# Opening stage of a diffusion backbone layer: tokens fetched first, squares taken per token, half columns first, three DMA queues

## The chip, the cores and the metric

The kernel runs on one core of one Trainium2 chip. The time is that of the core on the device, in microseconds (us): 2735.46 us as the median of 3 runs (2735.38 to 2736.6). A core has five engines with a program each: TensorE (PE), VectorE (DVE), ScalarE (ACT), GpSimd (POOL) and SyncE (SP), which here only issues DMAs. Each runs its own program in order and waits on semaphores for the others.

## The reference

One layer over 1024 latent tokens and 256 context tokens of width 1024, all in float32. Only the first part matters here: nine modulation rows per stream, then a norm with shift and scale, and the first SwiGLU network, whose hidden width is 2816.

```python
mod_lat = (silu(c) @ w_mod + b_mod)            # 9 rows of 1024: ml[0..8]
mod_ctx = (silu(c_ctx) @ w_mod + b_mod)        # mc[0..8]
x  = x  + 0.5 * ml[2] * swiglu(modulate(rms_norm(x,  norm1_g), ml[0], ml[1]), ffn1_w_in, ffn1_w_out)
cx = cx + 0.5 * mc[2] * swiglu(modulate(rms_norm(cx, norm1_g), mc[0], mc[1]), ffn1_w_in, ffn1_w_out)
hx = modulate(rms_norm(x, norm2_g), ml[3], ml[4])
...
return rms_norm(x, final_g)
```

Here `rms_norm(x, g) = x * rsqrt(mean(x*x) + eps) * g`, `modulate(h, shift, scale) = h * (1 + scale) + shift`, and `swiglu` is `(silu(a) * b) @ w_out` with `a, b` the two halves of `h @ w_in`. A convolution branch, attention, their merge and a second SwiGLU follow; they are the same in both kernels.

## The kernel before

**Numbers and products.** Everything is float32. A matrix that goes through PE is split into an upper part (rounded to fp32r, by a CAST on ScalarE) and a lower part (what is left, by a subtraction, mostly on VectorE), and each product term takes three matmuls (`terms`): upper by upper, upper by lower, lower by upper. A split weight lies in a tile `wh` or `wl` (the same thing in two pools of four buffers; the list `WH` says which of the first 16 goes where), its source in a `raw` tile of three buffers.

**Scheme.** The class `Winograd` forms the first network's two columns `a` and `b` of 128 for all 1024 tokens by seven products in place of eight. The 1024 features have an upper half (k 0 to 3) and a lower half (k 4 to 7), the tokens a first half C0 and a second half C1. The right-hand operands `r1` to `r7` are sums of the four blocks of the normed tokens: `r1` is the upper half of C0, `r2` its lower half, and `r3` to `r7` need C1 too. There are 22 units j, each of one column pair. Products 1 and 2 of a unit use column `a` alone; they are made for the first eight units ahead of everything (`start_together`, `AH1 = 8`), for these need only C0. Then each unit makes its products 6, 7, 4 (`second`) and 5, 3 (`third`). From unit 8 on the context's 256 tokens run beside a unit's weights (`SIDE_FROM = 8`); for units 0 to 7 they come in one pass of their own after unit 7.

**Opening.** A modulation half row is written (m, half): m = 1 is the scale, m = 0 the shift, half 0 its first 512 columns. For (1,0) and (0,0) `first_mod` makes both streams' rows on PE (`rawm` is the loaded weight, `silu_c` has two columns). For (1,1) and (0,1) `second_mod` makes the latent's alone, as sums on VectorE (`macc`) and a short product. The context's half of these comes later, in `later_mod`. The tokens of C0 (`xtok`, 128 tokens by 1024) are turned on PE, copied to `x`, squared on ScalarE (`sq`), summed by GpSimd (`sq_acc`), and a product with ones gives the sums per token. `rsqrt_cols` finds the root on VectorE by small steps (`rs_a`, `rs_y`, `rs_t`), and `bcast` turns it into a tile that VectorE multiplies by (`h0`); `shifted` then applies gain and shift on ScalarE, and `keep` splits into `r1`, `r2`. The same is done for C1, whose `norm1` makes `r3` to `r7` with `scaled`, sums and splits on VectorE.

**Work beside the units.** `all_later_mods` is a chain of small steps. After unit j, `STEPS[j]` of them run: none after unit 0, and 6, 6, 6, 7, 7, 8, 8 after units 1 to 7, 48 in all. A `later_mod` pass of one half row has 8 steps with loads and sums on VectorE, then waits, a split, and a short product on PE: 19 steps. The chain begins with (1,1) and (0,1) for the context, then the context's norm `normc` (10 steps; results `h1ch`, `h1cl`, the operands of the context products), then the rows m = 2 and up.

**Order.** All weights, tokens and modulation rows are fetched on SP's queue; the 16 stores of `x` to DRAM (`xd`) are on it too. The code is written in the order of the wanted program, and the tile scheduler then settles each engine's order by a time simulation of its own; on the chip an engine keeps that order.

The order of the opening and of the chain is set by these lines:

```python
    half1.prefetch(8, lo_engines=(dve, pool))
    raws11 = fetch_mod(1, 1)
    t1 = fetch_tokens(C1)
    half1.prefetch(10)
    raws01 = fetch_mod(0, 1)
    tx = fetch_tokens(CC)
    ...
    def all_later_mods():
        yield from later_mod(1, (1,), (1,))
        yield from later_mod(0, (1,), (1,))
        part_gain(gain1["c"], 0, "g1", "c", 4, 8)
        for _ in normc:
            yield
```

Of the kernel before, what the change touches and what calls it, by code (L numbers as in the profile page):

```python
# [18 lines left out]
P = 128  # L19
# [23 lines left out]
WAIT = 4  # L43
AH1, WH = 8, (4, 5, 6, 7, 10, 11, 14, 15)
RESIDENT, AH2, AH3 = 2, 9, 9
# [4 lines left out]
def tile_dit_layer(  # L50
# [249 lines left out]

    def fetch_mod(m, half):
        raws = []
        for kk in range(KD // 2):
            raw = atile("rawm", (P, 2, 512))
            o = m * D + half * 512
            load(out=raw[:], in_=w_mod[0, kk * 256 : (kk + 1) * 256, o : o + 512].rearrange("(a p) n -> p a n", p=P))
            raws.append(raw)
        return raws
# [155 lines left out]
    class Winograd:  # L464
# [6 lines left out]
        def __init__(self, xs, gain, mod, m, pairs, plain=False, ahead=3, side_from=None):  # L471

            self.xs, self.gain, self.mod, self.m, self.plain = xs, gain, mod, m, plain
            self.r = {i: [None] * 4 for i in range(8)}
            self.side_from = side_from  # L480
            self.n_ahead, self.side, self.started, self.n_left = ahead, None, [], 0
            self.n_squares, self.accs = {}, {}
            self.source, self.ready = self.lefts(pairs, side_from), []
# [44 lines left out]
        def norm1(self):  # L528
            y = rstd_cols(self.accs[C1], 512, D)
            yield  # L530
# [44 lines left out]
        def lefts(self, pairs, side_from):  # L575
# [100 lines left out]
        def start_together(self):  # L676

            n = self.n_ahead
            ws = [self.ready.pop(0) for _ in range(8)]
            ps = [ps_s() for _ in range(4)]  # L680

            def together(i, js, ps):
                for k in range(4):
                    for j in js:
                        self.terms(ps[j], ws[2 * j + i - 1], i, k)

            uc = {}
            for js in ((0, 1), (2, 3)):
                together(1, js, ps)
                for j in js:  # L690
                    uc[j] = atile("uc", (P, 2, 512))
                    act.copy(out=uc[j][:, 0], in_=ps[j])
                yield
            for j in range(4, n):
                p1 = self.product(1)
                uc[j] = atile("uc", (P, 2, 512))
                act.copy(out=uc[j][:, 0], in_=p1)
                yield
            for js in ((0, 1), (2, 3)):
                p2 = {j: ps_s() for j in js}  # L700
                together(2, js, p2)
                for j in js:
                    dve.tensor_add(out=uc[j][:, 1], in0=uc[j][:, 0], in1=p2[j])
                    self.started.append((uc[j][:, 0], uc[j][:, 1]))
                yield
            for j in range(4, n):
                dve.tensor_add(out=uc[j][:, 1], in0=uc[j][:, 0], in1=self.product(2))
                self.put_aside(uc[j])
                yield
# [218 lines left out]

    def fetch_tokens(ch):
        s, o, n = ch  # L930
        src = x[0] if s == "l" else ctxt[0]
        toks = []
        for j in range(n // P):
            t = atile("xtok")
            load(out=t[:], in_=src[o + j * P : o + (j + 1) * P, :])
            toks.append(t)
        return toks
# [28 lines left out]

    def squares(ch, turn):

        accs = [ttile("sq_acc")]
        for k in range(KD):  # L970
            run(turn, 1)
            sq = ttile("sq") if k else accs[0]
            act.activation(out=sq, in_=xs(k, ch), func=AF.Square)
            if k == KD - 1:
                accs.append(sq)
            elif k:
                pool.tensor_add(out=accs[0], in0=accs[0], in1=sq)
            yield accs

    run(mod10, 2)  # L980
    for accs in squares(C0, turn_tokens(C0, t0, ("dve", "dve"))):
        pass
# [9 lines left out]
    run(mod00, 1)  # L992
    y = rstd_cols(accs, 512, D)
    run(mod00)
    pr = bcast(y, 512)
    half1.h0 = h0 = [atile("h0", (P, 2, 512)) for _ in range(4)]

    def scaled(k, i):
        dve.tensor_mul(out=h0[k][:, i], in0=xs(k + 4 * i, C0), in1=pr)

    scaled(0, 0)
    scaled(1, 0)
    for k in range(4):
        half1.shifted(h0[k][:, 0], k)
        half1.keep(1, k, h0[k][:, 0])
        if k < 2:
            scaled(k + 2, 0)
# [3 lines left out]
    for k in range(4):  # L1011
        scaled(k, 1)
    run(mod11, 8)
    run(start, 2)
    turned = squares(C1, turn_tokens(C1, t1))
    run(mod11, 1)
    run(turned, 2)
    run(mod11, 1)
    for k in range(6):
        accs = next(turned)  # L1020
        run(mod01, 2 if k < 2 else 1)
    run(start, 2)
    half1.accs[C1] = accs
    norm1 = half1.norm1()
    run(mod11)
    part_gain(gain1["l"], 0, "g1", "l", 4, 8)
    run(mod01, 1)
    run(norm1, 1)
# [4 lines left out]
    run(norm1, 1)  # L1033
    run(start, 1)
    run(norm1, 1)
    run(start, 1)
    for _ in range(3):
        run(norm1, 1)
        run(start, 1)
    run(start)  # L1040
# [764 lines left out]
```

## Time and profile before

| what | before |
|---|---|
| median of 3 runs | 2735.46 us (2735.38 to 2736.6) |
| profiled execution, its span | 2735.6 us |
| PE busy | 2662.7 us, 97% |
| VectorE busy | 2021.2 us, 74% |
| ScalarE busy | 1152.3 us, 42% |
| GpSimd busy | 547.9 us, 20% |
| DMA, mean over the span | 130 GB/s |

The profile is that of one execution. All times in it count from the start of its span. A row of the order of time has the start, the busy time, the engine, the line (always L88, the helper that records every operation), the operation and its tiles (out<-in, buffer numbers left out), partitions by elements, a count, and in brackets the idle time before it with what ended it. Since every operation is at line 88, the tiles' names say which part of the kernel a row is. A row of the stretches has start and end, the length, the busy times, with how many instructions, and the granted clock of PE as a share of full speed. The page's digits show PE's idle time in the opening: 7, 8, 9, 8 tenths busy in the first four slices of 68 us, 9 in nearly all the others.

### The profile page before, as it was taken

The numbers are of one execution on the slowest core, as the hardware profiler recorded it, in microseconds if no ns is written. First come the engines' busy times: TensorE is split into PE (matmuls) and PEld (weight loads), VectorE is DVE, ScalarE is ACT, GpSimd is POOL, SyncE is SP. The second block draws the span as 40 slices with busy tenths as digits, with TensorE's granted clock in tenths as the row PEclk, the third lists the DMA queues.
The fourth block names the chain that finished last, engine by engine and source line by source line (L and its number), as shares of the span: only waits on it lengthen the run. The fifth ranks groups of instructions, "written<-read, shape, count | busy, mean of one in ns | idle before, by whom it ended". The sixth has DMA issues, their size and how long they took to land.

```text
span 2735.6 us, 37415 instructions
## 1 busy us (share of the span) xinstructions
PE 2662.7 (97%) x13629; PEld 2246.2 (82%) x13629; DVE 2021.2 (74%) x3368; ACT 1152.3 (42%) x2293; POOL 547.9 (20%) x419
## 2 busy tenths in 40 slices
PE   7898999999999999999999999999999999999998
PEld 4687988888878877888999888887888788888888
DVE  5887688877778799887578676685548886667885
ACT  4534333333444552333345566674226333334443
POOL 2241122221011024332023111100000442320200
PEclk8899999999999999999999999999999999999999
DMA  8264443434985255443312321001533552328841
GB/s 304 94 203 149 143 133 101 133 107 150 319 235 111 98 163 173 142 127 107 122 39 70 108 80 48 28 32 47 168 108 125 169 169 82 96 85 282 180 89 62
DMA packets 355650, 354.38 MB, mean 130 GB/s; under 512 B 27382, under 2 KB 248712, under 8 KB 355464
## 3 DMA queue, kind: packets, MB, share of 16 engines
q1 hardware_dynamic: 346440, 334.68, 37.5%
q0 software_dynamic: 9024, 17.30, 4.0%
q8 instruction: 107, 1.75, 0.3%
q14 instruction: 79, 0.65, 0.1%
HBM read 287.91 MB, written 63.96 MB: 129 GB/s over the span
## 4 chain that ended last, share of the span: by engine, by line
PE 55%; DVE 4%; ACT 1%; issue 1%; DMA 1%; POOL 0%; DVEq 0%; SPq 0%; POOLq 0%; ACTq 0%
PE ps L88 46%; PE pt L88 5%; PE po L88 4%; DVE wl L88 1%; DVE y L88 0%; DVE macc L88 0%; DVE u L88 0%; DVE ol L88 0%; ACT pts L88 0%; DVE v L88 0%; DVE r L88 0%; POOL s L88 0%; DVE x L88 0%; DVE pts L88 0%; DMA rawm<-in_w_mod_dram 0%
## 5 line engine op out<-in xcount | busy, mean ns | idle before, releaser
L88 PE MATMUL ps<-r,wl 128*128 128x512 f32 x5280 | 1231.3, 392 | 17.9 <-ACT r L88 6.1
L88 PEld LDWEIGHTS ps<-r,wl 128*128 128x128 f32 x5280 | 991.1, 189 | 232.4 <-DVE wl L88 8.7
L88 ACT CAST wl<-s 128x512 fp32r<-128x512 f32 x256 | 158.0, 620 | 344.2 <-PE ps L88 251.2
L88 POOL TENSOR_TENSOR s<-raw 128x512 f32<-128x512 f32 x64 | 99.8, 1559 | 944.0 <-DMA raw<-in_ffn_w_in_dram 575.3
L88 ACT CAST wl<-raw 128x512 fp32r<-128x512 f32 x278 | 171.7, 620 | 266.6 <-PE ps L88 172.8
L88 DVE TENSOR_TENSOR wl<-raw,wl 128x512 fp32r<-128x512 f32 x276 | 198.3, 719 | 80.8 <-ACT wl L88 79.5
L88 DVE TENSOR_TENSOR wl<-s,wl 128x512 fp32r<-128x512 f32 x256 | 222.1, 868 | 10.8 <-ACT wl L88 9.3
L88 POOL TENSOR_TENSOR s<-raw,s 128x512 f32<-128x512 f32 x64 | 104.7, 1636 | 415.3 <-DVE wl L88 415.3
L88 DVE SCALAR_TENSOR_TENSOR macc<-rawm,silu_c,macc 128x512 f32<-128x512 f32 x168 | 144.6, 879 | 9.5 <-DMA rawm<-in_w_mod_dram 8.8
L88 PE MATMUL ps<-wh,r 128*128 128x256 f32 x768 | 141.6, 285 | 0.0
L88 DVE TENSOR_TENSOR pts<-pt,pts 128x512 fp32r<-128x512 f32 x160 | 108.9, 687 | 39.3 <-ACT pts L88 38.4
L88 DVE TENSOR_TENSOR u<-u,ps 128x512 f32<-128x512 f32 x168 | 114.3, 680 | 30.9 <-PE ps L88 30.1
L88 DVE TENSOR_REDUCE m<-ps 128x1 f32<-128x512 f32 (+1 forms) x192 | 111.0, 596 | 30.8 <-PE ps L88 30.0
L88 ACT CAST pts<-pt 128x512 fp32r<-128x512 f32 x160 | 93.3, 594 | 88.7 <-PE pt L88 86.8
L88 PE MATMUL ps<-rh,wl 128*128 128x512 f32 x360 | 123.2, 392 | 2.8 <-ACT rh L88 2.8
L88 ACT CAST rh<-hid 128x512 fp32r<-128x512 f32 x132 | 81.1, 620 | 97.9 <-PE ps L88 78.9
L88 PEld LDWEIGHTS ps<-wh,r 128*128 128x128 f32 x768 | 120.6, 192 | 0.0
L88 PE MATMUL po<-pts,vh 128*128 128x512 f32 x256 | 110.5, 437 | 1.5 <-ACT pts L88 1.5
L88 PE MATMUL ps<-wl,r 128*128 128x256 f32 x384 | 108.8, 283 | 0.0
L88 ACT CAST wh<-raw 128x512 fp32r<-128x512 f32 (+1 forms) x84 | 67.1, 803 | 97.2 <-PE ps L88 76.3
L88 PE MATMUL ps<-kl,qs 128*128 128x512 f32 x384 | 105.3, 397 | 0.0
L88 DVE TENSOR_TENSOR rl<-hid,rh 128x512 fp32r<-128x512 f32 x132 | 90.0, 686 | 20.1 <-PE ps L88 12.2
(281 smaller groups left out, 5112.6 us busy)
## 6 DMA issues: line engine op xcount, KB each, us to landing
raw<-in_ffn_w_in_dram SPq DMA_DIRECT2D x117, 512.0 KB, 5.0
raw<-in_ffn_w_out_dram SPq DMA_DIRECT2D x72, 512.0 KB, 5.6
rawm<-in_w_mod_dram SPq DMA_DIRECT2D x128, 256.0 KB, 4.4
raw<-in_w_in_dram SPq DMA_DIRECT2D x61, 512.0 KB, 3.7
hid<-hd SPq DMA_DIRECT2D x40, 512.0 KB, 7.0
ws<-in_ffn_w_out_dram POOLq DMA_DIRECT2D x30, 512.0 KB, 6.6
hd<-c SPq DMA_DIRECT2D x38, 256.0 KB, 2.0
hd<-u SPq DMA_DIRECT2D x38, 256.0 KB, 2.8
```

The costliest lines, as they stand in the source:

```text
L88: inst = getattr(self.engine, name)(*args, **kw)
```

## The change

The opening is written anew, and one pass of the chain goes:

- **Fetches.** C0's tokens are fetched ahead of (1,0) and (0,0). `load`, `fetch_mod` and `fetch_tokens` take a queue: (1,1), C1's tokens and (0,1) are now issued by ScalarE, the 16 stores of `x` by GpSimd. The context's tokens are fetched later, still on SP.
- **Squares.** `token_rstd` squares a token tile of 1024 on ScalarE, with the row sum in the same instruction (`sqtok`, `rs_a`), straight after it is fetched. `squares`, GpSimd's sums and the product with ones are gone.
- **Scaling.** The broadcast root is copied to SBUF (`pr`). Each turned block is scaled from PSUM into `h0` by VectorE, while ScalarE copies it to `x`.
- **Weights.** The 16 columns for products 1 and 2 are all loaded as halves, the upper halves of the eight pairs first, then the lower ones; before, four were whole columns and came first. `start_together` follows that order: units 0 and 1 together, then one unit at a time. `WH` is adapted.
- **Modulation.** (1,1) is made on PE for both streams (`first_mod`), with the context's gain behind it, so the chain's first pass `later_mod(1, (1,), (1,))` is gone; with the same `STEPS`, all that follows in the chain runs 19 steps earlier. (0,1) is still made by `second_mod`.
- **Second half.** C1's root comes from `token_rstd`; its tokens are turned behind the first lower-half products rather than between the upper ones.

```diff
-    def load(out, in_, pinned=False):
-        inst = sp.dma_start(out=out, in_=in_)
+    def load(out, in_, pinned=False, queue=None):
+        inst = (queue or sp).dma_start(out=out, in_=in_)
...
             n = self.n_ahead
-            m = 4 if self.side_from else n
-            for a, _ in pairs[:m]:
-                yield from map(parts, cols(a))
-            for half in range(2):
-                for a, _ in pairs[m:n]:
-                    yield parts(half_cols(a, half))
+            if self.side_from:
+                for half in range(2):
+                    for a, _ in pairs[:n]:
+                        yield parts(half_cols(a, half))
+            else:
+                for a, _ in pairs[:n]:
+                    yield from map(parts, cols(a))
...
-    raws10 = fetch_mod(1, 0)
     t0 = fetch_tokens(C0)
-    raws00 = fetch_mod(0, 0)
+    raws10, raws00 = fetch_mod(1, 0), fetch_mod(0, 0)
...
+    def token_rstd(toks):
+
+        ss, sq = small("rs_a", 4), atile("sqtok")
+        for j, t in enumerate(toks):
+            act.activation(out=sq[:], in_=t[:], func=AF.Square, accum_out=ss[:, j : j + 1])
+        dve.tensor_scalar(out=ss[:], in0=ss[:], scalar1=D * EPS, scalar2=None, op0=ALU.add)
+        return rsqrt_cols(ss[:], 4)
+
+    half1.prefetch(3)
+    y = token_rstd(t0)
+    raws11 = fetch_mod(1, 1, act)
+    pr = ttile("pr")
+    dve.tensor_copy(out=pr, in_=bcast(y, 512))
+    half1.h0 = h0 = [atile("h0", (P, 2, 512)) for _ in range(4)]
+    run(mod10, 1)
+    for k in range(KD):
+        pt = (ps_o if k % 2 else ps_t)()
+        for j, t in enumerate(t0):
+            transpose(pt[:, j * P : (j + 1) * P], t[:, k * P : (k + 1) * P])
+        act.copy(out=xs(k, C0), in_=pt)
+        dve.tensor_mul(out=h0[k % 4][:, k // 4], in0=pt, in1=pr)
     run(mod10)
     for s in "lc":
         part_gain(gain1[s], 0, "g1", s, 0, 4)
-    half1.prefetch(8, lo_engines=(dve, pool))
-    raws11 = fetch_mod(1, 1)
-    t1 = fetch_tokens(C1)
-    half1.prefetch(10)
-    raws01 = fetch_mod(0, 1)
-    tx = fetch_tokens(CC)
+    t1 = fetch_tokens(C1, act)
+    raws01 = fetch_mod(0, 1, act)
+    half1.prefetch(5, lo_engines=(dve, pool))
...
     start = half1.start_together()
     run(start, 2)
-    mod11, mod01 = second_mod(1, 1, raws11), second_mod(0, 1, raws01)
...
+    mod11, mod01 = first_mod(1, 1, raws11), second_mod(0, 1, raws01)
     run(mod11)
     part_gain(gain1["l"], 0, "g1", "l", 4, 8)
+    part_gain(gain1["c"], 0, "g1", "c", 4, 8)
+    run(start, 1)
+    run(mod01, 8)
+    run(start, 2)
+    half1.rstd1 = token_rstd(t1)
     run(mod01)
     for k in range(4):
         half1.shifted(h0[k][:, 1], k + 4)
         half1.keep(2, k, h0[k][:, 1])
+    run(start, 2)
+    tx = fetch_tokens(CC)
+    run(turn_tokens(C1, t1, ("act", "dve")))
+    norm1 = half1.norm1()
     run(start, 1)
+    run(norm1, 2)
+    for _ in range(4):
+        run(start, 1)
         run(norm1, 1)
...
-            sp.dma_start(out=xd[k, :, ch[1] : ch[1] + 512], in_=xs(k, ch))
+            pool.dma_start(out=xd[k, :, ch[1] : ch[1] + 512], in_=xs(k, ch))
...
     def all_later_mods():
-        yield from later_mod(1, (1,), (1,))
         yield from later_mod(0, (1,), (1,))
-        part_gain(gain1["c"], 0, "g1", "c", 4, 8)
         for _ in normc:
             yield
```

**ScalarE in the opening.** These rows are ScalarE's program from the first modulation row to the splits of the first weights, before; the numbers at names are buffers, and the brackets hold the semaphores that a row waits for (DMAHW: the completion of DMAs).

```order
L88 COPY mrow_139<-ps_130 2x512 [waits PE_49]
L88 ACTIVATE sq_acc_141<-x_147 128x512 [waits DVE_49]
L88 ACTIVATE sq_157<-x_155 128x512 [waits DVE_49]
L88 ACTIVATE sq_167<-x_165 128x512 [waits DVE_49]
L88 ACTIVATE sq_177<-x_175 128x512 [waits DVE_49]
L88 ACTIVATE sq_186<-x_147 128x512
L88 CAST wl_228<-raw_226 128x512 [waits DMAHW0_49]
L88 CAST wl_231<-raw_226 128x512
```

The same place after the change, and, behind the "...", the rows between the third weight's split and the first shift.

```order
L88 ACTIVATE sqtok_146,rs_a_145<-xtok_110 128x1024 [waits DMAHW7_49,Activation_49]
L88 DMA rawm_164<-in_w_mod_dram 128x2x512 [waits DMAHW3_49]
L88 DMA rawm_166<-in_w_mod_dram 128x2x512 [waits DMAHW4_49]
...
L88 CAST wl_142<-raw_140 128x512 [waits DMAHW2_49]
...
L88 DMA xtok_267<-in_x_dram 128x1024 [waits DMAHW3_49]
L88 DMA xtok_269<-in_x_dram 128x1024 [waits DMAHW4_49]
L88 DMA xtok_271<-in_x_dram 128x1024 [waits DMAHW5_49]
L88 COPY x_211<-pt_236 128x512 [waits PE_49]
L88 DMA rawm_273<-in_w_mod_dram 128x2x512 [waits DMAHW6_49]
L88 COPY x_203<-po_229 128x512 [waits PE_49]
```

The squares are now of whole token rows and stand ahead of the weights' splits; twelve DMA issues, each waiting for the transfer eight before it, and the copies of `x` have come into ScalarE's line ahead of the shifts.

**PE at the second token half's norm.** Before, PE's rows around the broadcast of C1's root (`pt_678<-ident,rs_y_639`), which stands ahead of the first product of the lower half (`r_150` is an `r2`):

```order
L88 MATMUL ps_651<-accl_625,ones_r 1x512
L88 MATMUL pt_656<-ident,mrow_654 128x1 x4
L88 MATMUL pt_678<-ident,rs_y_639 128x128 x4
L88 MATMUL pt_939<-ident,xtok_292 128x128
L88 MATMUL pt_939<-ident,xtok_294 128x128
L88 MATMUL ps_683<-r_150_663,wl_231 128x512
L88 MATMUL ps_684<-r_150_663,wl_239 128x512
```

After, the same broadcast (`pt_650<-ident,rs_y_473`; `r_106` to `r_109` are the four `r2`):

```order
L88 MATMUL ps_612<-r_109_513,wl_449 128x512
L88 MATMUL ps_613<-r_109_513,wl_519 128x512 x3
L88 MATMUL ps_655<-r_108_509,wl_539 128x512 x3
L88 MATMUL ps_655<-r_109_513,wl_539 128x512 x3
L88 MATMUL ps_708<-r_106_501,wl_616 128x512
L88 MATMUL pt_650<-ident,rs_y_473 128x128 x4
L88 MATMUL ps_708<-r_106_501,wl_616 128x512 x2
```

It has moved behind the lower-half products of units 0 to 2 and one of unit 3.

**VectorE at the context's root.** Before, the root's first row (`rs_a_1873<-pt_1870`) stands at the end of unit 7, among its last adds to `u` and splits of weights:

```order
L88 TENSOR_TENSOR u_1725<-u_1725,ps_1951 128x512
L88 TENSOR_TENSOR wl_1966<-raw_1926,wl_1966 128x512
L88 TENSOR_SCALAR rs_a_1873<-pt_1870 128x2
L88 TENSOR_SCALAR rs_y_1875<-rs_a_1873 128x2
L88 SCALAR_TENSOR_TENSOR rs_t_1876<-rs_y_1875 128x2
```

After, it stands in unit 5, with the norm's first rows (`nt`) behind it and ahead of the unit's next add (`v_1608`):

```order
L88 TENSOR_TENSOR wl_1628<-s_311_1467,wl_1628 128x512
L88 TENSOR_TENSOR modc<-mcol_1535,bcol 128x4
...
L88 TENSOR_SCALAR rs_a_1567<-pt_1564 128x2
L88 TENSOR_SCALAR rs_y_1569<-rs_a_1567 128x2
...
L88 TENSOR_TENSOR nt_1584<-xc_97,pt_1581 128x256
L88 TENSOR_TENSOR nt_1589<-xc_97,pt_1581 128x256
L88 TENSOR_TENSOR nt_1594<-xc_97,pt_1581 128x256
L88 TENSOR_TENSOR nt_1599<-xc_97,pt_1581 128x256
L88 TENSOR_SCALAR nt_1584<-nt_1584,gain_c,modc 128x256
L88 TENSOR_TENSOR v_1608<-u_1421,ps_1631 128x512
```

The root, its eleven small rows and the context's norm have moved two units ahead, between the adds and splits of units 5 and 6.

More of the change, by code (lines that the diff above doesn't have):

```diff
@@ L43 @@
 WAIT = 4
-AH1, WH = 8, (4, 5, 6, 7, 10, 11, 14, 15)
+AH1, WH = 8, (4, 5, 6, 7, 12, 13, 14, 15)
 RESIDENT, AH2, AH3 = 2, 9, 9
@@ L299, in later_mod, with fetch_mod @@
             yield
-    def fetch_mod(m, half):
+    def fetch_mod(m, half, queue=None):
         raws = []
@@ L305, in fetch_mod @@
             o = m * D + half * 512
-            load(out=raw[:], in_=w_mod[0, kk * 256 : (kk + 1) * 256, o : o + 512].rearrange("(a p) n -> p a n", p=P))
+            src = w_mod[0, kk * 256 : (kk + 1) * 256, o : o + 512].rearrange("(a p) n -> p a n", p=P)
+            load(raw[:], src, queue is not None, queue)
             raws.append(raw)
@@ L528, in norm1 @@
         def norm1(self):
-            y = rstd_cols(self.accs[C1], 512, D)
+            y = self.rstd1 or rstd_cols(self.accs[C1], 512, D)
             yield
@@ L678, in start_together, with together @@
             n = self.n_ahead
-            ws = [self.ready.pop(0) for _ in range(8)]
-            ps = [ps_s() for _ in range(4)]
-            def together(i, js, ps):
+            uc = [None] * n
+            def together(i, js):
+                ps = [ps_s() for _ in js]
+                ws = [self.left() for _ in js]
                 for k in range(4):
[L684 to L690, printed above, removed]
+                    for w, p in zip(ws, ps):
+                        self.terms(p, w, i, k)
+                return zip(js, ps)
+            groups = ((0, 1), *((j,) for j in range(2, n)))
+            for js in groups:
+                for j, p in together(1, js):
                     uc[j] = atile("uc", (P, 2, 512))
-                    act.copy(out=uc[j][:, 0], in_=ps[j])
+                    act.copy(out=uc[j][:, 0], in_=p)
                 yield
[L694 to L708, printed above, removed]
+            for js in groups:
+                for j, p in together(2, js):
+                    dve.tensor_add(out=uc[j][:, 1], in0=uc[j][:, 0], in1=p)
+                    if j < 4:
+                        self.started.append((uc[j][:, 0], uc[j][:, 1]))
+                    else:
+                        self.put_aside(uc[j])
                 yield
@@ L927, in tile_dit_layer, with fetch_tokens @@
     xs, xc = Latents("x"), Context("xc")
-    def fetch_tokens(ch):
+    def fetch_tokens(ch, queue=None):
         s, o, n = ch
@@ L934, in fetch_tokens @@
             t = atile("xtok")
-            load(out=t[:], in_=src[o + j * P : o + (j + 1) * P, :])
+            load(t[:], src[o + j * P : o + (j + 1) * P, :], queue is not None, queue)
             toks.append(t)
@@ L965, in tile_dit_layer @@
     half1 = Winograd(xs, gain1["l"], modl, 0, column_pairs(ffn1_w_in[0], ffn_offsets), ahead=AH1, side_from=SIDE_FROM)
[L967 to L982, printed above, removed]
+    def token_rstd(toks):
[17 more added lines that the diff above has]
+        dve.tensor_mul(out=h0[k % 4][:, k // 4], in0=pt, in1=pr)
     run(mod10)
@@ L1005, in tile_dit_layer @@
         half1.keep(1, k, h0[k][:, 0])
-        if k < 2:
-            scaled(k + 2, 0)
+    half1.prefetch(8, lo_engines=(dve, pool))
     start = half1.start_together()
     run(start, 2)
-    mod11, mod01 = second_mod(1, 1, raws11), second_mod(0, 1, raws01)
[L1011 to L1024, printed above, removed]
+    mod11, mod01 = first_mod(1, 1, raws11), second_mod(0, 1, raws01)
     run(mod11)
     part_gain(gain1["l"], 0, "g1", "l", 4, 8)
-    run(mod01, 1)
-    run(norm1, 1)
+    part_gain(gain1["c"], 0, "g1", "c", 4, 8)
[3 more added lines that the diff above has]
+    half1.rstd1 = token_rstd(t1)
     run(mod01)
```

15 lines of the change are left out of this document (1 added, 14 removed).

## The prediction

> **What bounds the kernel now.** I read the page's head, then busy time in stretches cut where the program's stages begin and end, then the order of time around each gap of TensorE (PE).
>
> ```profile
> span 2735.6 us, 37415 instructions
> ...
> 0.00:44.40 44.40, 28.93 (x103) 12.83 (x103) 22.60 (x47) 14.57 (x25) 13.16 (x15) 0.87 0.98 361
> 44.40:71.40 27.00, 26.43 (x114) 21.30 (x115) 16.32 (x22) 14.42 (x28) 4.62 (x3) 0.90 0.59 196
> 71.40:88.20 16.80, 8.80 (x43) 6.51 (x41) 11.49 (x27) 9.63 (x18) 5.93 (x4) 0.66 0.44 141
> 112.90:127.90 15.00, 11.57 (x42) 7.17 (x40) 14.28 (x19) 5.41 (x10) 8.38 (x4) 0.89 0.57 194
> 180.80:234.00 53.20, 53.05 (x235) 42.79 (x233) 43.36 (x72) 18.69 (x36) 18.72 (x12) 1.00 0.54 167
> 234.00:244.00 10.00, 1.59 (x5) 0.91 (x6) 9.13 (x31) 3.89 (x10) 0.00 (x0) 0.67 0.39 124
> 244.00:320.00 76.00, 71.86 (x571) 70.72 (x571) 46.98 (x78) 35.46 (x68) 6.33 (x4) 0.98 0.49 159
> 320.00:700.00 380.00, 379.66 (x2122) 330.48 (x2121) 295.39 (x453) 128.37 (x231) 84.97 (x52) 1.00 0.41 129
> ```
>
> Columns: stretch, length, busy PE, weight loads, VectorE (DVE), ScalarE (ACT), GpSimd (POOL), granted clock, DMA share, GB/s. PE is the bound from 320 us on (379.66 of 380); what is late there stays late. So the change is worth what it moves in the first 245 us. PE does little useful before 44.4 us, little from 71.4 to 88.2 and almost nothing from 234 to 244. The profiled span, 2735.6, is 0.14 above the median of the runs shown (2735.46), so the sum is made against 2735.6.
>
> ```profile
> 32.29 0.38 PE L88 MATMUL pt<-ones,sq_acc 128*128 128x1 f32 x2 [4.49 <-POOL sq_acc L88]
> 40.47 1.09 PE L88 MATMUL pt<-ident,rs_y 128*128 128x128 f32 x4 [3.69 <-DVE rs_y L88]
> 44.39 1.22 PE L88 MATMUL ps<-r,wl 128*128 128x512 f32 x2 [1.56 <-ACT r L88]
> 88.21 1.22 PE L88 MATMUL ps<-r,wl 128*128 128x512 f32 x2 [1.40 <-ACT r L88]
> 136.96 54.28 PE L88 MATMUL ps<-r,wl 128*128 128x512 f32 x238
> 237.24 0.60 PE L88 MATMUL pt<-ident,rs_y 128*128 128x128 f32 x2 [3.29 <-DVE rs_y L88]
> 241.43 0.58 PE L88 MATMUL ps<-h1ch,wl 128*128 128x256 f32 x1 [3.59 <-ACT h1ch L88]
> 243.59 0.58 PE L88 MATMUL ps<-h1cl,wl 128*128 128x256 f32 x1 [1.58 <-DVE h1cl L88]
> ```
>
> Three waits stand out. The first product starts at 44.39, after GpSimd's sum of squares (4.49) and VectorE's root (3.69). The second half's products start at 88.21. At 234 PE waits for the context norm: 3.29 + 3.59 + 1.58 = 8.5. A 512-wide product matmul takes 54.28 / 238 = 0.228.
>
> **The change, part by part.** The old opening first.
>
> ```profile
> 6.00:50.00 44.00, 33.31 (x114) 16.19 (x115) 27.73 (x52) 15.55 (x27) 14.03 (x10) 0.81 1.06 397
> q1 hardware_dynamic: 11944, 18.21, 98.4%
> 6.33 0.43 SPq L88 DMA_DIRECT2D rawm<-in_w_mod_dram  x1
> ...
> 10.13 0.37 SPq L88 DMA_DIRECT2D rawm<-in_w_mod_dram  x1
> 22.50 2.16 ACT L88 CAST wl<-raw 128x512 fp32r<-128x512 f32 x4
> 6.38 9.85 PE L88 MATMUL ps<-rawm,silu_c 128*2 128x512 f32 x16 [2.51 <-DMA rawm<-in_w_mod_dram]
> ```
>
> *Fetches.* One queue holds the 16 DMA engines full (share 1.06, 397 GB/s). The four issues of SP from 6.33 to 10.13 (first and last shown) stand 1.27 apart: each waits for the transfer eight before it, the first of which is the one PE reads at 6.38. So 512 KB land every 1.27, from 6.3 on. After the change the four token tiles land from 6.3 to 10.1 and the modulation columns (1,0) and (0,0) next; the first split of a weight follows the same twelve transfers, as it does now at 22.5. But ScalarE's queue now puts 2.1 MB of (1,1) beside them. The third half weight is the 9.2nd MB: 8.7 MB after the first tile, 21.9 at 397 GB/s, ends at 28; with (1,1) left behind it would be at 23. I take 26.
>
> The Trainium skill, "DMA: Bandwidth & Descriptors", section "Issuing engines are not separate DMA queues", speaks against the three queues: transfers of SP, ScalarE and GpSimd run on the same 16 engines and interleave, and only issue time is saved. The rows above agree (98.4% with one queue). Were the queues to add bandwidth instead, the weights would come at 23 and the sum below would be 3 lower.
>
> *The first product.* Squares, root, broadcast and the first two of the eight scalings move ahead of the weights: they end near 17, beside the fetches, so GpSimd's sums (4.49) and most of the root's wait go. What is late next is ScalarE's own line. Behind the third weight stand, in its order, 11 casts and copies, 8 DMA issues, 4 shifts and a cast.
>
> ```profile
> 47.22 1.13 ACT L88 CAST wh<-raw 128x512 fp32r<-128x512 f32 x2
> 84.73 2.93 ACT L88 ACTIVATE h<-h,modl,gain_l 128x512 f32<-128x512 f32 x4 [0.87 <-DVE modl L88]
> L88 ACT ACTIVATE ws<-ws x12: 632/1057/1062, 779.3 to 2577.5; 128x1024 f32<-128x1024 f32 x10, 128x512 f32<-128x512 f32 x2
> L88 POOL DMA_DIRECT2D ws<-in_ffn_w_out_dram x36: 1197/1222/1442, 740.3 to 2624.9; - x36
> ```
>
> Sum: 11 x 0.55 = 6.1, 8 x 0.42 = 3.3 (a DMA issued by ScalarE is not in this trace; SP's rows say 0.37 to 0.43, and up to 1.27 when the transfer eight before is late), 2.9 and 0.6: 12.9. The first product starts at 39, against 44.39. The squares with their row sums are not in the trace; the nearest row is 1.06 for a 1024-wide ACTIVATE, and four of them keep pace with tiles 1.27 apart. The 16 stores leave SP's queue for GpSimd's, at 1.2 each, and cost nothing on the path: behind them stand three of its splits, whose lower parts PE reads more than 10 us after the first product's start. Without that cover each would cost 1.2.
>
> *First to second half.*
>
> ```profile
> 70.20 0.93 PE L88 MATMUL pt<-ident,xtok 128*128 128x128 f32 x7
> 86.42 1.29 DVE L88 TENSOR_TENSOR h<-x,pt 128x512 f32<-128x512 f32 x2 [1.27 <-PE pt L88]
> 132.54 0.68 DVE L88 TENSOR_TENSOR r<-nt,r 128x512 fp32r<-128x512 f32 x1
> 86.40:133.20 46.80, 41.97 (x154) 31.53 (x154) 44.72 (x65) 25.53 (x44) 12.59 (x7) 0.85 0.20 68
> 105.07 1.41 DVE L88 TENSOR_TENSOR r<-h,r 128x512 fp32r<-128x512 f32 x1
> ```
>
> From 39 PE does 8 two-row products for (1,1), 9.85 / 16 x 8 = 4.9, 96 matmuls, 21.9, and about 1.5 at half clock: 67. Now this ends at 71.4. Then row, turn, add, 4 shifts and a cast, 4.5: the second half starts near 72, not 88.2. But that is not the gain. The second token half's norm is now broadcast behind 37 of these matmuls (8.4), 16 turns (16 x 0.93 / 7 = 2.1) and a cold start (1.7), so VectorE's first scaling comes at 84, against 86.42.
>
> From there VectorE is the bound, now as after: 65 instructions in 46.8 up to the last operand r of the first unit (133.2), 0.72 each, with some of them stretched (1.41 where 0.68 is usual). The new order has 58: 41.5, so 125.5. PE, done with the second half at 97, waits for it; that wait takes the place of the one at 71. **First term: 125.5 - 133.2 = -7.7.** Between: -13 (weights at 23, 3 less; 0.68 in place of 0.72 each, 2.3 less) and 0 (ScalarE's issues at 1.27 each: 6.9 more).
>
> *The context norm.* The column half (1,1) now comes for both streams at once, so a context pass of 19 steps goes, and the norm, which needed all 48 steps of units 1 to 7, is done by step 29, in unit 5. The gap at 234 goes, and with it the slow start behind it: the mean clock of 0.98 from 244 to 320 is a loss of 0.02 x 76 = 1.5. **Second term: -(8.5 + 1.5) = -10.** With the pass go 2.1 MB of SP's loads and its sums on VectorE, in units 1 to 3, where PE is full anyway: nothing.
>
> *What it is traded for.* The work of that gap, and half of the next modulation row, fall into units 4 to 7, where PE is full.
>
> ```profile
> 237.88 2.74 DVE L88 TENSOR_TENSOR nt<-xc,pt 128x256 f32<-128x256 f32 x8 [0.70 <-PE pt L88]
> 240.53 2.67 DVE L88 TENSOR_SCALAR nt<-nt,gain_c,modc 128x256 f32<-128x256 f32 x8
> 243.12 2.76 DVE L88 TENSOR_TENSOR h1cl<-nt,h1ch 128x256 fp32r<-128x256 f32 x8
> L88 DVE SCALAR_TENSOR_TENSOR macc<-rawm,silu_c,macc 128x512 f32<-128x512 f32 x14 | 13.4, 954 | 1.2 <-DMA rawm<-in_w_mod_dram 1.1
> ```
>
> VectorE gets 2.74 + 2.67 + 2.76 = 8.2 of norm, 2.2 of root (11 at 0.2), 7 more sums of modulation at 0.95 = 6.7 and 1.2 of others: 18.3. It was busy 43.4 of 53.2 there, so 8.5 do not fit. The root also stands in VectorE's line ahead of unit 5's adds: it waits for a sum that PE makes only in unit 5's last product, and behind it are queued the adds that free PE's banks and the splits of unit 6's weights. The splits run some four weights ahead of PE, which may hide part. **Third term: +9**, between 0 (all hidden) and +13.5 (another 5 for the root's wait). The 10 is thus nearly given back.
>
> Sum: 2735.6 - 7.7 - 10 + 9 = **2726.9**.
>
> The Trainium skill, "TensorE: Matmul & The Clock Gate", Part 1, says that an idle window of some 3.4 us puts PE back to half clock. By that rule PE's broken work from 97 to 125 would leave it cold and add about 1.7 to the sum; the stretch from 112.9 to 127.9, also broken, kept 0.89, so I add nothing.
>
> **The rivals.** *The backlog is hidden:* four weights of lead and unit 4's slack take the third term to 2, and the time is 2719.9. For it: VectorE has idle time in units 0 to 4. Against: its line is in order. *The opening gives nothing:* the weights come at 28 and ScalarE's issues cost double, the first term is -1, and the time is 2733.6; the queues bring nothing, then, and the change does not do what it says. For it: a full DMA, and the broadcast that is put late. *Slower:* ScalarE is held by its own fetches. Its eight later issues each wait for a transfer eight before; if its queue gets half the rate, a transfer is 2.6 apart, and 8 x 2.6 = 21 take the place of 3.3. The first product comes at 56.5, everything behind it 17.5 later, the first term is +9.8 and the time 2744.4. It decides for slower once the first product comes after some 53. Against it: by the time of its second four, the first four have landed.
>
> **How the numbers follow.** A measurement of this kernel tells about 0.2%, 5.5 us, from no change. Forecast 0.48 (0.42 of it faster by more), hidden backlog 0.20 (faster), nothing in the opening 0.20 (within), held ScalarE 0.12 (0.09 slower, 0.03 within). So faster 0.62, same 0.29, slower 0.09. The range goes from 2714 (a hidden backlog with early weights) to 2738, which leaves out the worst of the last rival.
>
> **What would show it.** First product near 39 and second half near 72; VectorE's first scaling of the second tokens near 84 and the last r of unit 0 near 125; no wait for rs_y or h1ch ahead of the first context product, but waits of PE for wl from VectorE in units 5 to 7, some 9 in all. If those are under 3, the third term is wrong; if ScalarE sits idle ahead of its DMA issues after 26 us, the first is.

## The result, and the profile after

The changed kernel is slower: 2758.97 us median of 4 runs (2757.08 to 2760.13) against 2736.03 (2735.38 to 2741.92), a ratio of 1.0082 (95% interval 1.0067 to 1.0096). Its profiled execution has a span of 2757.3, 21.7 more than before. That lies outside the range on record.

The page of the changed kernel shows the span and a new DMA queue, q10, which is ScalarE's; q1 is SP's and q0 GpSimd's.

```profile
span 2757.3 us, 37301 instructions
...
q10 hardware_dynamic: 2752, 6.29, 0.6%
```

The next view is the order of time on TensorE (PE): from the first product to the context pass, every row that waited for 2 us or more, and the start of the unbroken stretch.

```profile
51.14 1.65 PE L88 MATMUL ps<-r,wl 128*128 128x512 f32 x3 [2.04 <-ACT r L88]
...
88.68 5.49 PE L88 MATMUL ps<-r,wl 128*128 128x512 f32 x12 [2.82 <-ACT r L88]
...
127.21 5.70 PE L88 MATMUL ps<-r,wl 128*128 128x512 f32 x13 [8.09 <-ACT wl L88]
...
149.15 54.25 PE L88 MATMUL ps<-r,wl 128*128 128x512 f32 x238 [0.25 <-DVE wl L88]
...
223.49 16.42 PE L88 MATMUL ps<-r,wl 128*128 128x512 f32 x60 [4.53 <-ACT wl L88]
...
243.57 1.53 PE L88 MATMUL ps<-r,wl 128*128 128x512 f32 x4 [3.66 <-ACT wl L88]
...
281.91 2.07 PE L88 MATMUL ps<-hidc,wo 128*128 128x256 f32 x8 [9.54 <-ACT wo L88]
```

The first product comes at 51.14 in place of 44.39, the unbroken stretch of 238 products at 149.15 in place of 136.96. Then there are new waits in units 5 and 6 and one of 9.54 in the context pass. The long stretch behind all this is as before:

```profile
320.00:700.00 380.00, 378.26 (x2177) 332.07 (x2176) 288.39 (x439) 128.06 (x232) 87.04 (x55) 1.00 0.38 120
```

Why the first product is late stands in ScalarE's order of time (ACTq: its DMA issues).

```profile
29.19 0.83 ACTq L88 DMA_DIRECT2D xtok<-in_x_dram  x2
...
31.87 0.39 ACTq L88 DMA_DIRECT2D rawm<-in_w_mod_dram  x1
...
33.07 12.03 ACTq L88 DMA_DIRECT2D rawm<-in_w_mod_dram  x3
45.14 0.62 ACT L88 CAST wl<-raw 128x512 fp32r<-128x512 f32 x1 [11.49 <-DMA rawm<-in_w_mod_dram]
...
47.66 2.92 ACT L88 ACTIVATE h<-h,modl,gain_l 128x512 f32<-128x512 f32 x4
```

The last three of its eight later issues take 12.03 us; the splits, copies and shifts of the first operands stand behind them. Here are the three one by one, with two issues of SP that came before them:

```profile
29.79 0.37 SPq L88 DMA_DIRECT2D raw<-in_ffn_w_in_dram  x1
...
30.55 0.37 SPq L88 DMA_DIRECT2D raw<-in_ffn_w_in_dram  x1
...
33.07 0.39 ACTq L88 DMA_DIRECT2D rawm<-in_w_mod_dram  x1
40.52 0.37 ACTq L88 DMA_DIRECT2D rawm<-in_w_mod_dram  x1
44.72 0.37 ACTq L88 DMA_DIRECT2D rawm<-in_w_mod_dram  x1
```

Two waits, of 7.06 and 3.83 us, lie between the three. The program hands the same eight semaphores in turn to the issues of SP and of ScalarE, and an issue waits until the transfer that had its semaphore before has landed. The kept trace names the semaphores: the issue at 40.52 waits for SP's half weight of 29.79, whose last part lands at 40.50, and the issue at 44.72 for SP's half weight of 30.55, which lands at 44.70. These are 256 KB each. What the queues moved from 33.07 to 44.72 (packets, MB, share of the 16 engines' time):

```profile
q10 hardware_dynamic: 1023, 2.55, 59.1%
q0 software_dynamic: 400, 1.31, 27.7%
q1 hardware_dynamic: 1056, 0.52, 15.3%
```

The engines were full, and SP's weights got 0.52 MB of it, beside 2.55 of ScalarE's own fetches and 1.31 of the stores of `x`. On VectorE (DVE) the first scaling of the second tokens is then at 102.53, against 86.42.

```profile
102.53 1.29 DVE L88 TENSOR_TENSOR h<-x,pt 128x512 f32<-128x512 f32 x2
...
144.78 0.68 DVE L88 TENSOR_TENSOR r<-nt,r 128x512 fp32r<-128x512 f32 x1
```

A yardstick for the stages is SP's order of time, where each unit's last store to `hd` (`hd<-uc` for the first units, `hd<-u` from unit 4 on) marks its end. Units 0, 4, 7 and 8 before:

```profile
143.12 0.32 SPq L88 DMA_DIRECT2D hd<-uc  x1
...
193.69 0.54 SPq L88 DMA_DIRECT2D hd<-u  x1
...
236.74 0.34 SPq L88 DMA_DIRECT2D hd<-u  x1
...
350.27 0.33 SPq L88 DMA_DIRECT2D hd<-u  x1
```

The same after:

```profile
155.19 0.34 SPq L88 DMA_DIRECT2D hd<-uc  x1
...
207.14 0.54 SPq L88 DMA_DIRECT2D hd<-u  x1
...
269.94 0.39 SPq L88 DMA_DIRECT2D hd<-u  x1
...
375.89 0.33 SPq L88 DMA_DIRECT2D hd<-u  x1
```

For the end of unit 7 this mark misleads, because the store follows VectorE and not PE. PE's last products of unit 7, before and after:

```profile
232.06 1.88 PE L88 MATMUL ps<-r,wl 128*128 128x512 f32 x7
```

```profile
257.60 2.46 PE L88 MATMUL ps<-r,wl 128*128 128x512 f32 x10
```

Before, PE ends the unit at 233.94 and the store comes 2.8 later. After, PE ends it at 260.06 and goes straight on with the context pass, while VectorE is behind and the store comes 9.9 later. So the stages are cut at PE's end of unit 7:

| from, to | before | after | difference | forecast |
|---|---|---|---|---|
| start to unit 0's last store | 143.12 | 155.19 | +12.1 | -7.7 |
| to unit 4's | 50.57 | 51.95 | +1.4 | 0 |
| to PE's last product of unit 7 (units 5, 6, 7) | 40.25 | 52.92 | +12.7 | +9 |
| to unit 8's last store (with the context pass) | 116.33 | 115.83 | -0.5 | -10 |
| to the end | 2385.3 | 2381.4 | -3.9 | 0 |

By unit 7's store the third and fourth row would read 43.05 to 62.80 (+19.8) and 113.53 to 105.95 (-7.6). The experiments below were planned with these; where it matters, PE's mark is given too.

### The profile page after: what moved, and what is told of

It is laid out like the page before. It is cut to its first block, busy times and chain, and to the rows that moved or that the text cites. A ratio compares the mean times of both kernels' runs of the same rounds, so it can differ in the third digit from the quotient of the medians.

```text
span 2757.3 us, 37301 instructions
## 1 busy us (share of the span) xinstructions
PE 2662.5 (97%) x13609; PEld 2237.9 (81%) x13609; DVE 1996.3 (72%) x3344; ACT 1155.3 (42%) x2298; POOL 537.9 (20%) x422
## 4 chain that ended last, share of the span: by engine, by line
PE 55%; DVE 3%; ACT 1%; DMA 1%; issue 1%; POOL 0%; DVEq 0%; ACTq 0%; POOLq 0%
PE ps L88 46%; PE pt L88 5%; PE po L88 4%; DVE xb L88 0%; DMA rawm<-in_w_mod_dram 0%; DVE ol L88 0%; DVE wl L88 0%; ACT pts L88 0%; DVE r L88 0%; DMA raw<-in_w_branch_conv_dram 0%; DVE x L88 0%; DVE pts L88 0%; DVE wc L88 0%; ACT pl L88 0%; ACT pc L88 0%
## 5 line engine op out<-in xcount | busy, mean ns | idle before, releaser
L88 DVE TENSOR_TENSOR wl<-s,wl 128x512 fp32r<-128x512 f32 x256 | 221.3, 865 | 13.8 <-ACT wl L88 12.0
L88 DVE SCALAR_TENSOR_TENSOR macc<-rawm,silu_c,macc 128x512 f32<-128x512 f32 x154 | 131.7, 874 | 11.2 <-DMA rawm<-in_w_mod_dram 10.7
```

What stands on the lines that cost most here:

```text
L88: inst = getattr(self.engine, name)(*args, **kw)
```

## The experiments

Times are medians; the ratio is to the kernel before, run beside it (2736.9 to 2739.9). Every profile is of one run; where it is far from its median this is said. "Units 5 to 7" goes from unit 4's store to unit 7's, unless PE's mark is named.

**1. The eight fetches later on ScalarE.**

```diff
-    t1 = fetch_tokens(C1, act)
-    raws01 = fetch_mod(0, 1, act)
     half1.prefetch(5, lo_engines=(dve, pool))
     run(mod00)
     for k in range(4):
         half1.shifted(h0[k][:, 0], k)
         half1.keep(1, k, h0[k][:, 0])
+    t1 = fetch_tokens(C1, act)
+    raws01 = fetch_mod(0, 1, act)
```

> The eight later fetches (four token tiles of the second half, four tiles of (0,1)) are issued by ScalarE behind the shifts and splits of the first operands, not ahead of them. Theory A (ScalarE is held 12.0 us by its own issues, from 33.07 to 45.1, and everything behind moves with it): first product at 39 to 41 in place of 51.1, second half at 77 in place of 88.7, unit 0's last hd store near 144 in place of 155.2, time about 12 less than the changed kernel, 2747. Rival B (the end of the opening is set by VectorE's scalings of the second tokens, which wait for a broadcast that stands behind 46 products, and not by the first product): first product at 40 all the same, but unit 0's store at 151 or later and the time less by 4 at most, 2755.

Measured: 2743.22 (2740.55 to 2749.43), ratio 1.0025 (1.0016 to 1.0035). PE's rows of this kernel:

```profile
37.26 1.65 PE L88 MATMUL ps<-r,wl 128*128 128x512 f32 x3 [2.46 <-ACT r L88]
38.84 8.60 PE L88 MATMUL ps<-rawm,silu_c 128*2 128x512 f32 x16
...
74.33 3.07 PE L88 MATMUL ps<-r,wl 128*128 128x512 f32 x12 [2.70 <-ACT r L88]
...
206.60 17.14 PE L88 MATMUL ps<-r,wl 128*128 128x512 f32 x60 [4.53 <-ACT wl L88]
...
226.26 13.42 PE L88 MATMUL ps<-r,wl 128*128 128x512 f32 x50 [2.52 <-ACT wl L88]
...
264.23 2.08 PE L88 MATMUL ps<-hidc,wo 128*128 128x256 f32 x8 [9.48 <-ACT wo L88]
```

The first product comes 13.9 earlier, unit 0's store at 138.24, 17 earlier, and the time is 15.8 less: theory A holds, B falls. The profile is of the fastest of ten runs (2740.55). The waits behind 200 us are still there, so they are another matter.

**2. The same eight fetches on SP.**

```diff
-    t1 = fetch_tokens(C1, act)
-    raws01 = fetch_mod(0, 1, act)
+    t1 = fetch_tokens(C1, sp)
+    raws01 = fetch_mod(0, 1, sp)
```

> The same eight fetches at the same place in the code, but issued by SP. Theory A: ScalarE isn't held, the first product comes at 39 to 42; but weights four and later now queue behind 4.2 MB, about 10 us at 400 GB/s, so PE waits in the first half: second half at 80 to 84, time 2748 to 2753. If it was the DMA's bandwidth and not the issuing engine that made the first product late (rival C), it stays at 48 to 51 and the time at 2757.

Measured: 2745.76, ratio 1.0029 (1.0019 to 1.0039).

```profile
37.25 1.65 PE L88 MATMUL ps<-r,wl 128*128 128x512 f32 x3 [2.46 <-ACT r L88]
...
74.81 5.49 PE L88 MATMUL ps<-r,wl 128*128 128x512 f32 x12 [2.70 <-ACT r L88]
```

The first product is where it was in experiment 1, with the fetches ahead of all weights but the first three: rival C (bandwidth) falls. The wait for the later weights that I expected did not come: the second half starts at 74.8, not at 80 to 84. So what was lost is the issuing engine's time: ScalarE's queue brought nothing for these fetches that SP's did not. The two half weights that ScalarE's issues had waited for are issued here at 29.52 and 30.19, ahead of the eight fetches in the same queue, and land at 32.24 and 35.04 by the kept trace, 2.7 and 4.9 after their issue in place of 10.7 and 14.2.

**3. The context's norm after unit 7 again.**

```diff
     def all_later_mods():
+        for _ in range(19):
+            yield
         yield from later_mod(0, (1,), (1,))
```

> The changed kernel with 19 empty steps at the head of the chain, so that the context's norm runs after unit 7 again, as before the change. Theory D (its root and sums in VectorE's line cost 21 us in units 4 to 7, and the gap of 8 to 10 us ahead of the context pass was cheaper): opening as in the changed kernel (unit 0's store at 155), units 4 to 7 take 43 between the u stores of units 4 and 7 as before the change (now 62.8), the gap of 8 to 10 comes back, time 2744 to 2747. Rival E (units 4 to 7 are late for another reason, fetches or the stores on GpSimd): those 62.8 stay above 55 and the time is at or above 2757.

Measured: 2744.95, ratio 1.0029 (1.0018 to 1.0039), 14 less than the changed kernel. Units 5 to 7 take 39.2 (205.12 to 244.34; 37.1 to PE's last product), and the old waits are back, as in the rows of before:

```profile
244.84 0.43 PE L88 MATMUL pt<-ident,rs_y 128*128 128x128 f32 x2 [2.63 <-DVE rs_y L88]
248.86 0.58 PE L88 MATMUL ps<-h1ch,wl 128*128 128x256 f32 x1 [3.59 <-ACT h1ch L88]
251.02 0.58 PE L88 MATMUL ps<-h1cl,wl 128*128 128x256 f32 x1 [1.58 <-DVE h1cl L88]
```

Theory D holds: moving the chain forward removed waits of 7.8 and cost 15.8 of PE's time in units 5 to 7 (52.9 less 37.1; by the stores 23.6).

**4. Both edits.**

> Both edits together. If theories A and D are independent, 12 and 12 add: about 2733, 2 to 3 below the kernel before. With rival B in place of A: 2741.

Measured: 2730.41 (2727.41 to 2733.96), ratio 0.9968 (0.9956 to 0.9981). The two causes add; the kernel is now faster than before. The profile is of its slowest run (2733.96).

**5. The norm early, the next row late.** From here on the late fetches of experiment 1 stay.

```diff
         for _ in normc:
             yield
+        for _ in range(19):
+            yield
```

> Base: the kernel with the eight late fetches (2743.2). 19 empty steps are put behind the context's norm, so that the norm stays in units 4 to 7 but the row (2,0) with its sums and its eight small DMAs runs after unit 7. Theory F (three prices: the root's place in VectorE's line, some 10 us in unit 5; the row's sums, some 8 in units 6 and 7; the row's eight small DMAs on SP ahead of the context's output weights, a PE wait of 9.5): unit 5 still takes 28 to 30 between u stores, units 6 and 7 fall from 16.9 and 15.5 to 12 or 13, the 9.5 wait for wo goes; time about 2726, below the kernel before. Rival G (the norm's own sums fill VectorE up to unit 7): units 6 and 7 stay at 15 to 17, only the 9.5 goes, 2734.

Measured: 2732.87 (2725.98 to 2737.81), ratio 0.9984 (0.9975 to 0.9994). Unit 5 takes 28.8, units 6 and 7 fall to 11.0 and 11.1 (experiment 1: 29.6, 16.9, 15.5), and the wait for `wo` is gone: the units follow theory F, not G, though the time fell by 10.4, not 17. What the row put in the way of `wo` is seen in SP's order of time in the changed kernel:

```profile
272.30 4.98 SPq L88 DMA_DIRECT2D mcol<-mrow  x8
277.32 1.07 SPq L88 DMA_DIRECT2D raw<-in_ffn_w_out_dram  x2
```

The eight small DMAs of the row (2,0) stand ahead of the context's output weights, which PE waits for until 281.91. From PE's last product of unit 7 to unit 8's store the time fell from 115.2 to 105.7, which is that wait of 9.48. In units 5 to 7, to PE's mark, the row's sums were worth only 3.2 (52.0 to 48.8): the 8 of theory F was read from the stores, which VectorE sets. 9.5 and 3.2 make 12.7, near the 10.4.

**6. Steps spread.**

```diff
-STEPS = (0, 6, 6, 6, 7, 7, 8, 8, 8, 12)
+STEPS = (0, 6, 6, 7, 4, 4, 4, 0, 8, 12)
```

> Same base; the steps per unit are 0, 6, 6, 7, 4, 4, 4, 0, so that the norm's steps are spread over units 4 to 6, four each, and the row (2,0) begins after unit 8. By theory F unit 5 takes 24 to 29 (the root's wait stays, two of the norm's feature blocks less), unit 6 13 to 15, unit 7 12, no wait for wo: about 2724. By rival G 2730 or more.

Measured: 2732.89, ratio 0.9982 (0.9973 to 0.9992). Units 5, 6, 7 take 22.7, 13.8 and 10.5 in the profile, which is of its fastest run (2723.86). The units went about as F said, each a little below; the time missed by 9 and equals experiment 5's: nothing was gained that the medians show.

**7. The second tokens' broadcast early** (base: experiment 4).

```diff
+    run(turn_tokens(C1, t1, ("act", "dve")))
+    norm1 = half1.norm1()
+    run(norm1, 2)
     for k in range(4):
         half1.shifted(h0[k][:, 1], k + 4)
         half1.keep(2, k, h0[k][:, 1])
     run(start, 2)
     tx = fetch_tokens(CC)
-    run(turn_tokens(C1, t1, ("act", "dve")))
-    norm1 = half1.norm1()
     run(start, 1)
-    run(norm1, 2)
```

> Base: late fetches and empty steps at the chain's head (2730.4). The second tokens are turned, and their root broadcast, ahead of the lower half's shifts in the code; on PE the turns then all stand ahead of the second half's products and the broadcast behind 27 of them in place of 46. If VectorE's first scaling of the second tokens sets the end of the opening (theory H), it moves from 88.7 to 85 and the time by 3 to 4, to 2727. Rival: the second half starts 2 later for the turns, and nothing is gained, 2730.

Measured: 2728.71 (2724.42 to 2730.82), ratio 0.9971 (0.9959 to 0.9983), 1.7 below experiment 4: inside what the two sets of runs share. In the profiles the first scaling moves from 88.69 to 83.44 and the unbroken stretch from 135.39 to 130.77, but 2.4 of that is PE's clock (last section), and the two profiles are of the slowest run of experiment 4 and the fastest of this kernel (2724.42). Inconclusive.

**8. The stores of x on SP** (base: experiment 4).

> Base as for x9 (2730.4); the 16 stores of x go back to SP's queue. If they cost nothing on the path on either queue, as the prediction put it, 2729 to 2732. If GpSimd's waits for them (67 us in the profile) delay its sums of weights, ahead of which PE waits 8.1 near 113, that wait goes or shrinks and the time falls by 3 to 8. If SP is the worse place, the first half's weights come later and the time rises by over 3.

Measured: 2730.2, ratio 0.9973 (0.9964 to 0.9983), and the wait of 8.09 near 111 is as long. The stores cost nothing on SP's queue that they do not cost on GpSimd's, with the fetches late; what they cost in the changed kernel, where they ran beside the held issues, was not tried.

**9. Sum and root apart** (base: experiment 5; seven of its empty steps move between sum and root).

```diff
         acc = sum_squares(xs, ch)
         yield
-        y = rstd_cols([acc], n, D)
+        pss = col_sums([acc], n)
+        for _ in range(gap):
+            yield
+        y = col_root(pss, n, D)
...
-    normc = modulated_norm(xc, *hc, CC, gain1, mods, 0)
+    normc = modulated_norm(xc, *hc, CC, gain1, mods, 0, 7)
```

> Base: late fetches, empty steps behind the context's norm (2732.9; unit 5 takes 28.8 between u stores against 19.4 before the change). In the first context norm alone seven steps are put between the product with ones and the root (and seven of the empty steps go), so that VectorE reaches the root's first row 8 rows of unit 6 later and no longer waits for PE's sum (5.29 in the changed kernel). If that wait and what is queued behind it is the price of unit 5 (theory F1), unit 5 falls to 20 to 23, units 6 and 7 take up the norm's sums and rise to 13 or 14 each, and the time falls by 3 to 6, to about 2728. If VectorE's added load is the price (F2), units 5 to 7 together stay at 50 to 52, only shifted, and the time at 2732.

Measured: 2720.36 (2719.08 to 2721.07), ratio 0.9933 (0.9914 to 0.9953), 12.5 below experiment 5. VectorE's order of time in experiment 5, with PE's product that it waits for, and then the root in this kernel:

```profile
201.38 0.50 PE L88 MATMUL pt<-ones,sq_acc 128*128 128x1 f32 x4
201.91 0.16 DVE L88 TENSOR_SCALAR rs_a<-pt 128x2 f32<-128x2 f32 x1 [5.29 <-PE pt L88]
...
210.03 16.89 PE L88 MATMUL ps<-r,wl 128*128 128x512 f32 x62 [4.53 <-ACT wl L88]
```

```profile
198.37 0.50 PE L88 MATMUL pt<-ones,sq_acc 128*128 128x1 f32 x4
201.06 0.14 DVE L88 TENSOR_SCALAR rs_a<-pt 128x2 f32<-128x2 f32 x1
```

The root finds its sum ready, and PE's wait of 4.53 is gone. Units 5 to 7 take 14.0, 21.4 and 8.9, together 44.3, against 51.0 in experiment 5 and 43.05 before the change; to PE's mark 39.6, 48.8 and 40.3. F1 holds, F2 falls: with its root later, the norm's own work costs PE nothing that shows. The gain is larger than I expected, and the units did not split as I had said (20 to 23 for unit 5, 13 or 14 for the others).

**10. and 11. What helped, put together.** Experiment 10 takes experiments 1, 6 and 7 and two steps between sum and root (in both context norms); experiment 11 takes 9 and 7.

> All that helped, in one kernel: late fetches, second tokens turned and broadcast early, two steps between the sum and the root, steps per unit 0, 6, 6, 7, 4, 4, 4, 0, no empty steps. If the prices add (opening 2 to 4 from the early broadcast, 2 to 6 from the root, none of the gap ahead of the context pass), the time is 2720 to 2726, 11 to 17 below the kernel before. If VectorE's load in units 5 to 7 is the price whatever the order, 2728 to 2731, no better than late fetches with the norm left where it was.

Measured: 2721.56 (2719.58 to 2724.29), ratio 0.9944 (0.993 to 0.9957).

> The kernel of the last run (2720.4: late fetches, seven steps between sum and root, empty steps behind the norm) with the second tokens turned and broadcast early. If the early broadcast is worth what its single test showed on the base with the norm after unit 7 (1.7 in the median, 4.6 in the start of PE's unbroken stretch, 135.39 to 130.77), the time is 2716 to 2719. If its gain there was only that PE did not fall to half clock at the start of the second half (12 products in 5.49 against 3.07), which the last run did not show either, nothing is gained: 2720.

Measured: 2718.78 (2715.11 to 2721.86), ratio 0.9937 (0.9923 to 0.995). Experiments 9, 10 and 11 can't be told apart; each is some 0.6% faster than the kernel before.

## Why the prediction was wrong

- **The first term, -7.7, came out at +12.1.** The step that failed is ScalarE's line: "8 DMA issues at 0.42 = 3.3". They took 14.3 in all (0.83 + 0.44 + 0.63 + 0.39 + 12.03), beyond even the 1.27 each that I put as the bound. That bound was read from one queue alone, where transfers land 1.27 apart; here three queues shared the engines. The rival "ScalarE is held by its own fetches" had the right place, with 0.12 as its chance and a first product at 56.5, and its sign, ScalarE idle ahead of its issues after 26 us, is in the trace. But the transfers that it waited for were not its own. The argument against the rival (by the second four, the first four have landed) was true of those four, which had landed by 28.5. It left out that the other issues wait for SP's weights, and that these share the engines with the fetches that ScalarE has just issued: they landed 10.7 and 14.2 after their issue, and 2.7 and 4.9 where those fetches stood behind them in one queue (experiment 2). What part the stores of `x` had in it was not tried. Experiments 1 and 2 showed what the hold cost: with the issues elsewhere the first product came at 37.3, near the 39 of the sum. That is in part luck, for the third weight's split began at about 29, not at 26, and the 3.3 for the issues was not spent there. The time came out slower although 51.1 is short of the 53 that the rival asked for, because the next term failed too.
- **Smaller faults in the same term.** "8 two-row products, 9.85 / 16 x 8 = 4.9" read 16 records as 16 products; a half row of (1,1) makes 16 such records and takes 8.60 (experiment 1). So the second half came at 74.3 there, 37.1 after the first product and not 33. And 58 instructions at 0.72 are 41.8, not 41.5.
- **What was right in it.** VectorE sets the end: from the first scaling to the last r of unit 0 it took 42.9 after the change (102.53 to 145.46), for 41.5 forecast and 46.8 before. Without the hold unit 0's store came at 138.2, 4.9 before the old one, of 7.7 forecast.
- **The second term, -10, was -0.5.** The waits for `rs_y` and `h1ch` went, as said. The step that failed is that nothing was put in their place: a wait of 9.54 for `wo` came, behind the row's small DMAs on SP's queue ahead of the output weights. I counted the row's loads and sums, not the eight DMAs at its end. With that wait gone (experiment 5) the stage takes 105.7, 10.6 less than before, so the -10 itself was right.
- **The third term, +9, was +12.7.** The size is near and the range (0 to 13.5) holds it, but the mechanism was wrong, so this is luck. The step that failed is the price by VectorE's load (18.3 us into 9.8 of slack, 8.5 that do not fit). To PE's mark, experiment 1 takes 52.0 in units 5 to 7, experiment 5 without the row 48.8, experiment 9 with the root later 39.6, the kernel before 40.3. So the row's sums cost 3.2 and the root's place 9.2, and the rest of the norm nothing that shows. The wait of the root behind PE's sum was in the prediction, as 5 at the far end of the range only. The signpost "waits of PE for wl, some 9 in all" came out at 8.7 (4.53 + 3.66 + 0.49). Of the 4.0 beyond it 2.7 is PE's clock, for which I had put nothing: the stretches of the changed kernel around those waits (columns as in the prediction) show it at 0.80 and 0.86, and 60 products from 223.49 take 16.42, where 0.228 each makes 13.7.

```profile
215.00:225.00 10.00, 4.84 (x21) 3.05 (x20) 8.75 (x25) 3.32 (x8) 2.71 (x2) 0.80 0.00 1
225.00:235.00 10.00, 10.00 (x38) 7.56 (x39) 9.62 (x19) 3.17 (x7) 1.39 (x1) 0.86 0.56 155
```

- **The rest of the program** took 3.9 less. Over the profiles of the experiments it varies from 2378.4 (experiment 6) to 2385.8 (experiment 8), not in step with the place of the chain; why was not tried.
- The Trainium skill, "DMA: Bandwidth & Descriptors", section "Issuing engines are not separate DMA queues", says that other issuing engines save issue time only. The trace agrees on the bandwidth: with three queues at work, from 15 to 29 us, the changed kernel moved 390 GB/s, where SP's queue nearly alone moved 397 before, from 6 to 50 us. Issue time on the path was not saved here but lost.

## What to carry to other kernels

A DMA issue on a computing engine stands in that engine's line, and where it waits for an earlier transfer, on another queue too, all behind it waits (7.06 and 3.83 here); put it behind the work that others wait for. A mark that follows one engine, such as a store, does not tell what another has lost. When a chain of side work is shortened, everything behind it moves forward: look at where its waits and small DMAs then stand in each engine's line, not only at the sum of its busy time. An operation that waits for a late product of another engine belongs some rows behind that product, since what is queued behind it pays too.

## What the hardware showed that I had not expected

Two programs with the same opening ran the same stretch at two clocks. Experiments 1 and 4 have the same opening; PE is idle for 2.70 us ahead of the second half in both, and for some 2 us before that it makes only turns and one-row products. The stretches of 3 us behind it (busy PE, weight loads, DVE, ACT, POOL, then the granted clock) in experiment 1, and then in experiment 4:

```profile
74.30:77.30 3.00, 2.97 (x13) 2.29 (x14) 2.99 (x5) 3.00 (x7) 0.56 (x1) 1.00 1.03 378
```

```profile
74.30:77.30 3.00, 2.39 (x6) 1.91 (x7) 2.41 (x4) 3.00 (x8) 0.56 (x1) 0.50 0.99 340
77.30:80.50 3.20, 3.20 (x10) 2.42 (x9) 0.69 (x2) 1.04 (x3) 1.08 (x2) 0.50 0.85 342
```

The first 12 products took 3.07 at clock 1.00 or 5.49 at 0.50. The Trainium skill, "TensorE: Matmul & The Clock Gate", Part 1, states that the clock falls after an idle window of about 3.4 us and that the window runs freely, so that its effect differs from run to run. The second agrees; a wait of 2.70, less than that window, came before half clock in these profiles, and whether the small products ahead of it had a part is not shown. In the prediction I added nothing for the clock. In the changed kernel, behind the wait of 8.09 near 119, 13 products took 5.70, where 0.228 each makes 3.0; VectorE sets the end of that stage, so what this cost is not known.
